# A hybrid encoder layer on one core: SyncE's and ScalarE's orders by hand in the recurrence, and 16 projection steps moved into it

## The chip, the core and the metric

The kernel runs on one core of a Trainium2 chip. TensorE (PE) multiplies, VectorE (DVE) and GpSimd (POOL) do elementwise work, ScalarE (ACT) does copies and activations, and SyncE (SP) issues most of the DMAs; ScalarE's queue issues some too. In the traces each engine takes its instructions in order, and a DMA that is issued on an engine's queue stands in that order as well. The metric is the time of one execution on the device in microseconds: before the change the median of three runs is 1126.07 us (1124.25 to 1127.57).

## What is computed

One layer with two branches is applied to two requests (1024 and 256 positions, 1280 in all, width 1024), with all arithmetic in float32 precision:

```python
h = rmsnorm(x) ; xs, zs, q, k, v, za, gs, ga = split(h @ w_in)      # 5120 columns
ys = s5_bidirectional(xs)            # 32 groups, 64 complex states, both directions
ys = gelu(ys) ; ys *= sigmoid(ys @ w_glu + b_glu) ; ys *= silu(zs)
ya = diff_attention(rotary(q), rotary(k), v)   # 4 heads, softmax1 - lam * softmax2
ya = rmsnorm(ya) * (1 - lam_init) * silu(za)
y  = x + (sigmoid(gs) * (ys @ wb0) + sigmoid(ga) * (ya @ wb1)) @ w_out ; rmsnorm(y)
```

## The kernel before

Float32 products are made of three fp32r products: each operand is split into a high part (a ScalarE cast) and a low part (a subtraction), and `hi*hi + hi*lo + lo*hi` is accumulated in PSUM.

The stages follow one another: norm and V projection; the projections of xs, q and k, with the tables of the recurrence prepared beside them; the recurrence (S5); attention, head by head; the tail behind attention (gate, preparation of both branches, merge, output projection). The 24 remaining projection tiles (zs, za, gs, ga) are no stage of their own: `filler_gen` (L699) is a generator that `fill(n)` (L721) advances by n steps wherever PE would wait. A step is three matmuls of some 424 columns (L706 to L708), eight steps make a chunk in one of two PSUM banks, three chunks make a tile: 576 steps. At a chunk's end ScalarE evicts the bank (`zo`, L712) and issues its store (L713). At the end of a tile's first chunk the weights two tiles ahead are loaded on ScalarE's queue (`w_stage`, L216) and split at once (`w_split`, L233: cast to `wh` at L239 on ScalarE, subtraction to `wl` at L240 on GpSimd). `wh` and `wl` have two buffers, so the cast waits until the tile two before is done.

The recurrence works on 8 blocks of 4 groups. For a block b: `in_mm` has 16 input products on PE (L776, L777), rotations on VectorE (L782 to L785) with two sums each on GpSimd; it also makes the decay table `rt` with four ScalarE activations (L770; two buffers, read by the scans). `scan` has four scans on VectorE (L797, L798) and six products that make `e` (L807 to L812). `out_mm` has 24 output products on PE (L825 to L827) and two gelu activations on ScalarE into `Y` (L828). `store_y` (L831) writes every second block's `Y` with eight DMAs. The order on PE and SP is that of the program (`tc.manual_schedule(engines={PE, SP})`); the other engines' order comes from a planner that simulates the kernel. In program order: loads, `fill(S_PRE=22)`, `in_mm(0)`, `fill(S_LEAD=10)`, and then for each b: loads, `scan(b)`, `in_mm(b+1)`, `fill(S_MID=13)`, `out_mm(b)`, `fill(S_END=4)`: 168 steps.

Attention takes 288 steps. `load_head` (L876) loads a head's q, k and v into the buffers of the recurrence (tags U, tb, mt, wcm, wb) as they come free; for the first head it stands behind the recurrence in the program, outside the hand order, so the planner places its loads among the recurrence's. `unit_scores` makes the scores of a query tile for two softmax terms: the first term needs q0, k00, k10, the second q1, k01, k11; `fill` steps are queued behind each term's score matmuls (L924, L926). The remaining 120 steps are issued by `fill(1000)` in the tail, where the buffers of attention have to come free before `glu_stage` and `ya_stage` can work; the merge products (L1058 to L1060) follow.

Of the kernel before, what the change touches and what calls it, by code (L numbers as in the profile page):

```python
# [11 lines left out]
F32 = mybir.dt.float32  # L12
F32R = mybir.dt.float32r
# [26 lines left out]
S_PRE, S_LEAD, S_MID, S_END = 22, 10, 13, 4  # L40
# [86 lines left out]
def kernel(  # L127
# [570 lines left out]

    def filler_gen():  # L699
        ws = [w_split(w_stage(tiles[0][1], A), G), w_split(w_stage(tiles[1][1], A), G)]  # L700
        for i, (dst, _) in enumerate(tiles):
            wh, wl = ws.pop(0)
            for ci, (c0, n) in enumerate(F_CHUNKS):
                ps = mm_bank()
                for k in range(KD):
                    PE.matmul(ps[:, :n], wh[:, k, :], hTh[:, k, c0:c0 + n], start=(k == 0), stop=False)  # L706
                    PE.matmul(ps[:, :n], wh[:, k, :], hTl[:, k, c0:c0 + n], start=False, stop=False)  # L707
                    PE.matmul(ps[:, :n], wl[:, k, :], hTh[:, k, c0:c0 + n], start=False, stop=(k == KD - 1))  # L708
                    if k < KD - 1:
                        yield  # L710
                zo = wp.tile([128, 512], F32, tag="zo", name="zo", bufs=3)
# [16 lines left out]
    sl = sl_ctx.enter_context(tc.tile_pool(name="s5l", bufs=1, side="right", reuse_waits="tile"))  # L728
    with ExitStack() as p2:
# [34 lines left out]

        def in_mm(b, tb, wb):
            q, gb = b // 2, (b % 2) * NB
            u = U[q]
            rt = sp_.tile([128, NB, J], F32, tag="rt", name="rt", bufs=2)
            for g in range(NB):
                A.activation(rt[:, g], rmask, AF.Copy, scale=r8[:, b * NB + g:b * NB + g + 1])  # L770
# [17 lines left out]
            return rt, bm  # L788
# [46 lines left out]
        with tc.manual_schedule(engines={mybir.EngineType.PE, mybir.EngineType.SP}):  # L835
# [7 lines left out]
            fill(S_PRE)  # L843
            cur = in_mm(0, tbs[0], wbs.pop(0))
            fill(S_LEAD)
            for b in range(NBLK):
# [11 lines left out]
                e = scan(b, tbs.pop(b), *cur)  # L858
# [5 lines left out]
                sig = out_mm(b, wcs.pop(b), e)  # L864
                fill(S_END)
            store_y(3)

    with tc.issue_after(sig.ins):
        tables = A.preload_act_table_set("natural_log_exp_and_others")
    with ExitStack() as p3:  # L870
# [4 lines left out]

        def load_head(h):  # L876
            pr, cb = h // 2, (h % 2) * 2
            big = lambda tag, b: sl.tile([128, NT], F32R, tag=tag, name=f"h{tag}", bufs=b)
            sml = lambda tag, b: sl.tile([128, LL], F32R, tag=tag, name=f"h{tag}", bufs=b)
            q0, k00, q1, vh = big("U", 2), big("tb", 2), big("tb", 2), big("U", 2)  # L880
            k10, k01, k11, vl, rest = sml("mt", 2), sml("wcm", 2), sml("wb", 1), sml("mt", 2), sml("wcm", 2)
            part = lambda i: rest[:, i * LS:(i + 1) * LS]
            v3 = lambda t: t.rearrange("p (k e) -> p k e", e=128)

            def load_q(t, q):
                rows = slice((cb + t) * 32, (cb + t) * 32 + 32)
                for s in range(2):
                    for f in range(2):
                        o = s * 64 + f * 32
                        SP.dma_start(q[o:o + 32].bitcast(F32), q_d[pr][s, f, rows])  # L890

            def load_k(t, hl, k, c0, n):
                rows = slice((cb + t) * 32, (cb + t) * 32 + 32)
                for s in range(2):
                    for f in range(2):
                        o = s * 64 + f * 32
                        SP.dma_start(k[o:o + 32].bitcast(F32), k_d[pr][hl, f, rows, c0:c0 + n])

            load_q(0, q0)
            load_k(0, 0, k00, 0, NT)  # L900
            load_k(0, 1, k10, 0, LL)
            load_q(1, q1)
            load_k(1, 0, k01, 0, LL)
            load_k(1, 1, k11, 0, LL)
            SP.dma_start(v3(vh).bitcast(F32), vh_d[h])
            SP.dma_start(v3(vl).bitcast(F32), vl_d[h][:, 0:8])
            load_k(0, 1, part(0), LL, LS)
            load_k(1, 0, part(1), LL, LS)
            load_k(1, 1, part(2), LL, LS)
            SP.dma_start(v3(part(3)).bitcast(F32), vl_d[h][:, 8:10])  # L910
            return (([q0[:, :LL], q1[:, :LL]], [k00[:, :LL], k01], [k10, k11], v3(vh)[:, 0:8], v3(vl)),
                    ([q0[:, LL:], q1[:, LL:]], [k00[:, LL:], part(1)], [part(0), part(2)],
                     v3(vh)[:, 8:10], v3(part(3))))
# [99 lines left out]
        for h in range(NH):  # L1013
            parts = load_head(h)
# [236 lines left out]
```

## Time and profile before

| | us |
|---|---|
| runs: median, lowest, highest | 1126.07, 1124.25, 1127.57 |
| profiled execution: its time, its span | 1127.2, 1125.1 |
| busy: PE, DVE, ACT, POOL | 1067.2, 801.0, 462.5, 354.8 |
| recurrence: first input product to last output product | 312.2 to 455.2 |
| attention | about 457 to 800 |
| last projection step | 871.2 |

A time in a profile row is counted from the span's start. Rows of a timeline give start, duration, engine, line and tiles; "x8" means that eight instructions in a row are merged, and a bracket tells how long the engine was idle before and which instruction ended that. ACTq and SPq are the queues' own steps, as the issue of a DMA. The granted clock of PE is a share of full speed: 1.0 is 2.4 GHz and 0.5 is 1.2 GHz; its mean over the span is 0.987.

### The profile page before, as it was taken

The numbers are of one execution on the slowest core, as the hardware profiler recorded it, in microseconds if no ns is written. First come the engines' busy times: TensorE is split into PE (matmuls) and PEld (weight loads), VectorE is DVE, ScalarE is ACT, GpSimd is POOL, SyncE is SP. The second block draws the span as 40 slices with busy tenths as digits, with TensorE's granted clock in tenths as the row PEclk, the third lists the DMA queues.
The fourth block names the chain that finished last, engine by engine and source line by source line (L and its number), as shares of the span: only waits on it lengthen the run. The fifth ranks groups of instructions, "written<-read, shape, count | busy, mean of one in ns | idle before, by whom it ended". The sixth has DMA issues, their size and how long they took to land.

```text
span 1125.1 us, 18000 instructions
## 1 busy us (share of the span) xinstructions
PE 1067.2 (95%) x6479; PEld 987.1 (88%) x6479; DVE 801.0 (71%) x1533; ACT 462.5 (41%) x927; POOL 354.8 (32%) x437
## 2 busy tenths in 40 slices
PE   5999799999989999999999999999999999998997
PEld 4878588788979988898999998989999999998997
DVE  5998997888579999478677777766442675666524
ACT  4453222332312121455555645554453445544332
POOL 2447999511032333122122222212141003520032
PEclk9999899999999999999999999999999999999999
DMA  7745453654596676615416316311645975569112
GB/s 212 170 141 188 142 174 117 209 166 156 173 282 174 205 202 168 177 51 150 141 47 169 122 47 186 114 40 60 210 124 174 292 230 128 167 194 270 48 57 94
DMA packets 186154, 173.59 MB, mean 154 GB/s; under 512 B 32721, under 2 KB 161745, under 8 KB 186066
## 3 DMA queue, kind: packets, MB, share of 16 engines
q1 hardware_dynamic: 150738, 144.13, 43.6%
q10 hardware_dynamic: 35328, 28.32, 7.9%
q8 instruction: 51, 0.84, 0.3%
q14 instruction: 37, 0.30, 0.1%
HBM read 113.71 MB, written 58.69 MB: 153 GB/s over the span
## 4 chain that ended last, share of the span: by engine, by line
PE 47%; DVE 18%; DMA 7%; ACT 4%; issue 3%; POOL 2%; SPq 0%; ACTq 0%; POOLq 0%; DVEq 0%
PE mm L706 5%; PE mm L707 5%; PE mm L708 5%; PE xb L1058 3%; PE xb L1059 3%; PE xb L1060 3%; PE pb L246 2%; PE pb L248 2%; PE pb L247 2%; DVE z L797 2%; DVE z L798 2%; PE S L924 2%; DMA yt<-ya_d 2%; PE S L926 2%; DVE mx L928 2%
## 5 line engine op out<-in xcount | busy, mean ns | idle before, releaser
L706 PE MATMUL mm<-hTh,wh 128*128 128x424 f32 (+1 forms) x576 | 212.2, 368 | 6.3 <-ACT zo L712 6.3
L708 PE MATMUL mm<-hTh,wl 128*128 128x424 f32 (+1 forms) x576 | 206.1, 358 | 0.0
L707 PE MATMUL mm<-hTl,wh 128*128 128x424 f32 (+1 forms) x576 | 206.0, 358 | 0.0
L706 PEld LDWEIGHTS mm<-hTh,wh 128*128 128x128 f32 x576 | 109.2, 190 | 12.6 <-ACT zo L712 8.1
L707 PEld LDWEIGHTS mm<-hTl,wh 128*128 128x128 f32 x576 | 109.2, 190 | 4.6
L708 PEld LDWEIGHTS mm<-hTh,wl 128*128 128x128 f32 x576 | 109.0, 189 | 3.4
L928 DVE TENSOR_REDUCE mx<-S 128x1 f32<-128x1024 f32 (+1 forms) x80 | 84.2, 1057 | 38.9 <-PE S L926 38.7
L939 POOL TENSOR_SCALAR p<-p,rs 128x1024 f32<-128x1024 f32 (+1 forms) x40 | 41.7, 1042 | 205.0 <-DVE rs L937 194.2
L246 PE MATMUL pb<-hTh,wh 128*128 128x512 f32 (+1 forms) x288 | 105.7, 367 | 0.0
L247 PE MATMUL pb<-hTl,wh 128*128 128x512 f32 (+1 forms) x288 | 105.1, 365 | 0.0
L932 ACT ACTIVATE p<-S,mx 128x1024 f32<-128x1024 f32 (+1 forms) x80 | 79.2, 992 | 63.0 <-DVE mx L929 53.8
L248 PE MATMUL pb<-hTh,wl 128*128 128x512 f32 (+1 forms) x288 | 103.9, 361 | 0.4 <-DVE wl L240 0.4
L240 POOL TENSOR_TENSOR wl<-wst,wh 128x1024 fp32r<-128x1024 f32 x24 | 64.3, 2679 | 126.5 <-ACT wh L239 51.7
L1191 PE MATMUL tr<-wqh,mh 128*128 128x256 f32 x320 | 89.7, 280 | 1.5 <-DVE o L1195 1.3
L1192 PE MATMUL tr<-wql,mh 128*128 128x256 f32 x320 | 89.3, 279 | 0.0
L1193 PE MATMUL tr<-wqh,ml 128*128 128x256 f32 x320 | 89.0, 279 | 0.0
L248 PEld LDWEIGHTS pb<-hTh,wl 128*128 128x128 f32 x288 | 54.6, 190 | 9.3 <-DVE wl L240 0.9
L246 PEld LDWEIGHTS pb<-hTh,wh 128*128 128x128 f32 x288 | 54.7, 190 | 8.6
L1191 PEld LDWEIGHTS tr<-wqh,mh 128*128 128x128 f32 x320 | 60.1, 188 | 2.4 <-DVE o L1195 2.4
L247 PEld LDWEIGHTS pb<-hTl,wh 128*128 128x128 f32 x288 | 54.6, 190 | 8.4
L1198 POOL TENSOR_TENSOR o<-o,finB 128x256 f32<-128x256 f32 x30 | 27.9, 934 | 103.8 <-ACT jk L1197 103.8
L1192 PEld LDWEIGHTS tr<-wql,mh 128*128 128x128 f32 x320 | 60.1, 188 | 0.0
(387 smaller groups left out, 2793.4 us busy)
## 6 DMA issues: line engine op xcount, KB each, us to landing
wst<-in_w_in_dram ACTq DMA_DIRECT2D x24, 512.0 KB, 4.0
wst<-in_w_in_dram SPq DMA_DIRECT2D x16, 512.0 KB, 4.8
wst<-in_w_branch_dram SPq DMA_DIRECT2D x32, 256.0 KB, 4.4
wqs<-in_w_out_dram SPq DMA_DIRECT2D x16, 512.0 KB, 3.8
tt_d<-tt SPq DMA_DIRECT2D x16, 320.0 KB, 2.6
tb<-tt_d SPq DMA_DIRECT2D x8, 640.0 KB, 5.1
zt<-gs_d SPq DMA_DIRECT2D x16, 320.0 KB, 4.3
x<-in_x_sample_dram SPq DMA_DIRECT2D x8, 512.0 KB, 4.6
```

Source lines behind the costliest of these rows:

```text
L240: e.tensor_tensor(lv, st, hv, op=ALU.subtract)
L246: PE.matmul(ps[:, :n], wh[:, k, :], hTh[:, k, c0:c0 + n], start=(k == 0), stop=False)
L247: PE.matmul(ps[:, :n], wh[:, k, :], hTl[:, k, c0:c0 + n], start=False, stop=False)
L248: PE.matmul(ps[:, :n], wl[:, k, :], hTh[:, k, c0:c0 + n], start=False, stop=(k == KD - 1))
L706: PE.matmul(ps[:, :n], wh[:, k, :], hTh[:, k, c0:c0 + n], start=(k == 0), stop=False)
L707: PE.matmul(ps[:, :n], wh[:, k, :], hTl[:, k, c0:c0 + n], start=False, stop=False)
L708: PE.matmul(ps[:, :n], wl[:, k, :], hTh[:, k, c0:c0 + n], start=False, stop=(k == KD - 1))
L928: V.tensor_reduce(mx, S[:, :nk], axis=AX.X, op=ALU.max)
L932: A.activation(p[:, :nk], S[:, :nk], AF.Exp, bias=mx, scale=1.0 / math.sqrt(HD), accum_out=sm[:, t:t + 1])
L1191: PE.matmul(ps[:, :256], mh[:, k, ts_], oh_[:, k], start=(k == 0), stop=False)
L1192: PE.matmul(ps[:, :256], mh[:, k, ts_], ol_[:, k], start=False, stop=False)
L1193: PE.matmul(ps[:, :256], ml[:, k, ts_], oh_[:, k], start=False, stop=(k == 7))
```

## The change

The order on ScalarE in the recurrence is now that of the program too. The decay tables leave `in_mm`: the first two are made behind `fill(S_PRE)`, table b+2 behind `out_mm(b)`. In the recurrence a weight tile's split is traced apart from its load: at the second step of the next tile (`apart`); during `fill(S_PRE)`, and in attention and the tail, it is traced at once, as before. The first head's loads become a generator `head(0, True)` that is advanced inside the hand order: q0 and k10 ahead of `scan(6)`, k11, k00 and k01 ahead of `scan(7)`, the rest behind the last `store_y`. S_LEAD goes from 10 to 18 and S_MID from 13 to 14, so 184 steps lie in the recurrence and 104 in the tail.

```diff
-S_PRE, S_LEAD, S_MID, S_END = 22, 10, 13, 4
+S_PRE, S_LEAD, S_MID, S_END = 22, 18, 14, 4
     def filler_gen():
         ws = [w_split(w_stage(tiles[0][1], A), G), w_split(w_stage(tiles[1][1], A), G)]
+        st = []
+        def split():
+            with tc.high_priority():
+                ws.append(w_split(st.pop(0), G))
...
+                    if st and (ci, k) == (0, 1):
+                        split()
                 zo = wp.tile([128, 512], F32, tag="zo", name="zo", bufs=3)
                 A.copy(zo[:, :n], ps[:, :n])
                 A.dma_start(dst[:, c0:c0 + n], zo[:, :n])
                 if ci == 0 and i + 2 < len(tiles):
                     with tc.high_priority():
-                        ws.append(w_split(w_stage(tiles[i + 2][1], A), G))
+                        st.append(w_stage(tiles[i + 2][1], A))
+                    if not apart[0]:
+                        split()
...
+    def head(h, staged=False):
...
+        q0 = big("U", 2)
+        load_q(0, q0)
+        if staged:
+            k10 = sml("mt", 2)
+            load_k(0, 1, k10, 0, LL)
+            yield
+            k11, k00, k01 = sml("wb", 1), big("tb", 2), sml("wcm", 2)
+            load_k(1, 1, k11, 0, LL)
+            load_k(0, 0, k00, 0, NT)
+            load_k(1, 0, k01, 0, LL)
+            yield
+            q1 = big("tb", 2)
+            load_q(1, q1)
...
+        vh, vl, rest = big("U", 2), sml("mt", 2), sml("wcm", 2)
...
+        def decay(b):
+            rt = sp_.tile([128, NB, J], F32, tag="rt", name="rt", bufs=2)
+            for g in range(NB):
+                A.activation(rt[:, g], rmask, AF.Copy, scale=r8[:, b * NB + g:b * NB + g + 1])
+            return rt
...
-        with tc.manual_schedule(engines={mybir.EngineType.PE, mybir.EngineType.SP}):
+        with tc.manual_schedule(engines={EN.PE, EN.SP, EN.Activation}):
...
             fill(S_PRE)
+            apart[0] = True
+            rts = [decay(0), decay(1)]
             cur = in_mm(0, tbs[0], wbs.pop(0))
             fill(S_LEAD)
+            first = head(0, True)
             for b in range(NBLK):
...
-                e = scan(b, tbs.pop(b), *cur)
+                if b >= NBLK - 2:
+                    next(first)
+                e = scan(b, tbs.pop(b), rts.pop(0), cur)
...
                 fill(S_MID)
                 sig = out_mm(b, wcs.pop(b), e)
+                if b + 2 < NBLK:
+                    rts.append(decay(b + 2))
                 fill(S_END)
             store_y(3)
+            first = next(first)
+        apart[0] = False
...
-            parts = load_head(h)
+            parts = next(head(h)) if h else first
```

## Rows read from the trace of the kernel before

**Rows 1.** The page, part 1: busy time, share of the span, instructions.
```profile
PE 1067.2 (95%) x6479; PEld 987.1 (88%) x6479; DVE 801.0 (71%) x1533; ACT 462.5 (41%) x927; POOL 354.8 (32%) x437
```
**Rows 2.** PE's waits, 298 to 480 us: total us, times, longest us.
```profile
PE mm L706 <- ACT zo L712: 5.8, 4, 2.3
PE tr L825 <- DVE e L809: 4.8, 1, 4.8
PE S L924 <- ACT p L932: 2.1, 1, 2.1
```
**Rows 3.** Table of stretches, 320 to 440 us: the sum, busy us of each engine.
```profile
sum 120.00, PE 111.46 PEld 107.60 DVE 113.83 ACT 24.15 POOL 39.05; mean PE 18.58 PEld 17.93 DVE 18.97 ACT 4.02 POOL 6.51
```
**Rows 4.** VectorE's timeline in the recurrence: some of the scans.
```profile
318.00 3.65 DVE L797 TENSOR_TENSOR_SCAN z<-rt,bm 64x640 f32<-64x640 f32 x1 [0.34 <-POOL bm L786]
...
404.97 2.15 DVE L797 TENSOR_TENSOR_SCAN z<-rt,bm 64x640 f32<-64x640 f32 x1 [0.33 <-POOL bm L786]
...
420.62 2.13 DVE L797 TENSOR_TENSOR_SCAN z<-rt,bm 64x640 f32<-64x640 f32 x1 [0.33 <-POOL bm L786]
...
427.84 1.49 DVE L798 TENSOR_TENSOR_SCAN z<-rt,bm 64x640 f32<-64x640 f32 x1
...
443.45 3.49 DVE L798 TENSOR_TENSOR_SCAN z<-rt,bm 64x640 f32<-64x640 f32 x1
```
**Rows 5.** GpSimd's timeline, 440 to 470 us: weight splits.
```profile
443.02 2.57 POOL L240 TENSOR_TENSOR wl<-wst,wh 128x1024 fp32r<-128x1024 f32 x1 [3.98 <-ACT wh L239]
458.79 2.39 POOL L240 TENSOR_TENSOR wl<-wst,wh 128x1024 fp32r<-128x1024 f32 x1 [13.20 <-PE S L926]
```
**Rows 6.** Table of stretches, L706 alone: us, PE busy (matmuls), PEld, clock, DMA.
```profile
862.00:871.40 9.40, 5.69 (x16) 2.98 (x16) 1.00 0.54 163
```
**Rows 7.** PE's timeline: first and last output products, scores, first merge product.
```profile
335.00 0.90 PE L825 MATMUL tr<-e,wcm 128*128 128x160 f32 x2 [4.84 <-DVE e L809]
...
341.75 0.46 PE L706 MATMUL mm<-hTh,wh 128*128 128x424 f32 x1
...
452.02 0.43 PE L825 MATMUL tr<-e,wcm 128*128 128x160 f32 x2
...
455.18 0.47 PE L706 MATMUL mm<-hTh,wh 128*128 128x424 f32 x1
...
460.88 0.63 PE L924 MATMUL S<-hwcm,htb 128*128 128x512 f32 x2
...
861.57 0.41 PE L1058 MATMUL xb<-ysh,wh 128*128 128x320 f32 x1 [0.42 <-ACT wh L1051]
```
**Rows 8.** ScalarE's timeline: start of the recurrence, and a store in attention.
```profile
304.92 2.67 ACT L770 ACTIVATE rt<-rmask,r 128x160 f32<-128x160 f32 x8
...
315.59 1.05 ACT L239 CAST wh<-wst 128x1024 fp32r<-128x1024 f32 x1 [6.68 <-PE mm L707]
316.54 0.51 ACT L712 COPY zo<-mm 128x424 f32<-128x424 f32 x1
322.03 0.34 ACTq L713 DMA_DIRECT2D zs_d<-zo  x1
...
468.94 0.33 ACTq L713 DMA_DIRECT2D za_d<-zo  x1
```
**Rows 9.** SyncE's timeline: loads at the recurrence's start and end.
```profile
309.67 11.51 SPq L747 DMA_DIRECT2D mt<-kt_d  x8
...
450.55 1.70 SPq L890 DMA_DIRECT2D htb<-q_d  x4
...
456.25 6.31 SPq L833 DMA_DIRECT2D gy_d<-Y  x8
```
**Rows 10.** Table of stretches: us, PE, PEld, DVE, ACT, POOL, granted clock, DMA.
```profile
334.70:341.50 6.80, 6.27 (x22) 5.87 (x23) 6.71 (x7) 0.44 (x1) 1.37 (x1) 0.50 0.42 155
471.24:474.65 3.41, 3.41 (x13) 2.97 (x11) 1.41 (x3) 0.00 (x0) 0.00 (x0) 0.50 0.14 36
```
**Rows 11.** Loads of q (L890), 430 to 470 us: from issue to landing.
```profile
DMA to landing us min/median/max: 2.6/3.1/5.7
```

More of the change, by code (lines that the diff above doesn't have):

```diff
@@ L697 @@
              + [(gs_d[i], O_GS + i * 128) for i in range(8)] + [(ga_d[i], O_GA + i * 128) for i in range(8)])
+    apart = [False]
     def filler_gen():
         ws = [w_split(w_stage(tiles[0][1], A), G), w_split(w_stage(tiles[1][1], A), G)]
+        st = []
+        def split():
+            with tc.high_priority():
+                ws.append(w_split(st.pop(0), G))
         for i, (dst, _) in enumerate(tiles):
@@ L728, with load_q, load_k @@
     sl = sl_ctx.enter_context(tc.tile_pool(name="s5l", bufs=1, side="right", reuse_waits="tile"))
+    def head(h, staged=False):
+        pr, cb = h // 2, (h % 2) * 2
+        big = lambda tag, b: sl.tile([128, NT], F32R, tag=tag, name=f"h{tag}", bufs=b)
+        sml = lambda tag, b: sl.tile([128, LL], F32R, tag=tag, name=f"h{tag}", bufs=b)
+        part = lambda i: rest[:, i * LS:(i + 1) * LS]
+        v3 = lambda t: t.rearrange("p (k e) -> p k e", e=128)
+        def load_q(t, q):
+            rows = slice((cb + t) * 32, (cb + t) * 32 + 32)
+            for s in range(2):
+                for f in range(2):
+                    o = s * 64 + f * 32
+                    SP.dma_start(q[o:o + 32].bitcast(F32), q_d[pr][s, f, rows])
+        def load_k(t, hl, k, c0, n):
+            rows = slice((cb + t) * 32, (cb + t) * 32 + 32)
+            for s in range(2):
+                for f in range(2):
+                    o = s * 64 + f * 32
+                    SP.dma_start(k[o:o + 32].bitcast(F32), k_d[pr][hl, f, rows, c0:c0 + n])
+        q0 = big("U", 2)
[11 more added lines that the diff above has]
+            load_q(1, q1)
+        else:
+            k00, q1 = big("tb", 2), big("tb", 2)
+            k10, k01, k11 = sml("mt", 2), sml("wcm", 2), sml("wb", 1)
+            load_k(0, 0, k00, 0, NT)
+            load_k(0, 1, k10, 0, LL)
+            load_q(1, q1)
+            load_k(1, 0, k01, 0, LL)
+            load_k(1, 1, k11, 0, LL)
+        vh, vl, rest = big("U", 2), sml("mt", 2), sml("wcm", 2)
+        SP.dma_start(v3(vh).bitcast(F32), vh_d[h])
+        SP.dma_start(v3(vl).bitcast(F32), vl_d[h][:, 0:8])
+        load_k(0, 1, part(0), LL, LS)
+        load_k(1, 0, part(1), LL, LS)
+        load_k(1, 1, part(2), LL, LS)
+        SP.dma_start(v3(part(3)).bitcast(F32), vl_d[h][:, 8:10])
+        yield (([q0[:, :LL], q1[:, :LL]], [k00[:, :LL], k01], [k10, k11], v3(vh)[:, 0:8], v3(vl)),
+               ([q0[:, LL:], q1[:, LL:]], [k00[:, LL:], part(1)], [part(0), part(2)],
+                v3(vh)[:, 8:10], v3(part(3))))
@@ L767, in in_mm @@
             u = U[q]
-            rt = sp_.tile([128, NB, J], F32, tag="rt", name="rt", bufs=2)
-            for g in range(NB):
-                A.activation(rt[:, g], rmask, AF.Copy, scale=r8[:, b * NB + g:b * NB + g + 1])
             bm = sp_.tile([128, 2, NB, J], F32, tag="bm", name="bm", bufs=2)
@@ L787, in in_mm @@
                 G.tensor_tensor(bm[:, 1, gsl], bm[:, 1, gsl], t2, op=ALU.subtract)
-            return rt, bm
+            return bm
         def scan(b, tb, rt, bm):
@@ L874 @@
         grp = [None]
[L876 to L913, printed above, removed]
         def unit_scores(hd, qi, nk, fu):
```

## The prediction

> **What bounds the kernel now.** I read the page first: TensorE (PE) is busy 95% of the span [rows 1], so the time is PE's work plus what PE loses. Its work is the same in both kernels: the 576 projection steps (three matmuls each) are only placed elsewhere. So I looked for where PE loses time. The table of PE's waits between 298 and 480 us [rows 2] shows 4.8 us at the first output product (L825) for VectorE's `e`, 5.8 us in four waits for a ScalarE eviction (`zo`, L712) and 2.1 us at a score matmul (L924). The recurrence is the stretch to ask about.
>
> There VectorE, not PE, sets the pace. The table of stretches over 320 to 440 us has DVE busy 113.8 of 120 us, PE 111.5 [rows 3]. VectorE's timeline shows the blocks as a chain of scans: the block that starts at 404.97 is followed by one at 420.62, 15.65 us later [rows 4]. A block in which a weight split (`wl`, L240) runs on GpSimd is longer: the same scan (L798) takes 1.49 us alone and 3.49 us beside the split that starts at 443.02 [rows 4, 5]. So 15.7 us without a split, 17.7 with one. PE needs less. A projection step is 0.58 us (16 in 9.4 us [rows 6]); 17 of them are 9.9 us; the 24 output products take 3.2 us (452.02 to 455.18 [rows 7]), and the 16 input products at the same rate 2.1: 15.2 us a block. With 18 steps it is 15.8 us, still under VectorE's mean of about 17.2 (three splits in four blocks).
>
> **The change part by part.**
>
> *Sixteen steps move (8 in S_LEAD, 1 in each of 8 S_MID).* They leave the tail behind attention, where the table of stretches counts exactly 16 L706 matmuls, so 16 steps, between 862.0 and 871.4 us [rows 6]: 9.3 us. What is late when they go? The first merge product, at 861.57, waited 0.42 us for a ScalarE cast [rows 7], so the chain of preparations that the tail covers ends just where those 16 steps begin. I take -9.0; the ends are -9.3 and 0 (if that chain grows by as much). In the recurrence the steps fill time in which PE waits for VectorE; that costs nothing as long as VectorE sets the end. If PE set it, they would cost their 9.3 us there.
>
> *Decay tables and ScalarE's hand order, steady blocks.* A block has four `rt` activations, 1.3 us together (eight are 2.67 us [rows 8]). Before, they stood in front of evictions and waited for the scan that frees their buffer; now they follow the output product's gelu, when that scan is long over, and are due a block later. The evictions no longer queue behind them, so the 5.8 us of `zo` waits [rows 2] go. Worth: nothing by itself. The wait for `e` is late next, and VectorE does not wait for PE there.
>
> *Decay tables and hand order, at the start: a loss.* Before, all eight `rt` activations ran from 304.92 on, in time that ScalarE had free [rows 8]. Now their place is behind fill(22). In that fill the split of weight tile 2 is still traced at once, behind the first chunk's eviction and ahead of the second's. Its cast waits until PE has done with tile 0, until 315.59 [rows 8], and the second chunk's eviction, that eviction's store and then the decay tables queue behind it. The store is the trouble. In the trace the eviction of 316.54 is over by 317.05, but its store is issued only at 322.03 [rows 8], after SyncE's eight `mt` loads, issued from 309.67 to 321.18 [rows 9]; ScalarE stood still until then. With the same place in the order the first four tables end at 322.03 + 0.33 + 1.33 = 323.7, against the first scan's start at 318.00 [rows 4]: +5.7 us. If the store is not held, 317.05 + 0.33 + 1.33 = 318.7: +0.7. Off go about 1.5 us: the first scan of 3.65 us, beside the split of tile 2, becomes one of 2.15 us [rows 4], as that split is then over. On come 2.0: the split of tile 8, at 458.79 before [rows 5], moves to step 170, into the last block. For the end of VectorE's last `e` I take +5.0, near the upper end, as the held store stands at this very place in the trace; the ends are -0.8 and +6.2.
>
> Here a rule speaks against the change. The scan beside the split is 2.0 us longer [rows 4, 5]. The Trainium skill (SBUF — State Buffer, Who interferes with whom) says that a VectorE instruction with two SBUF inputs and a GpSimd instruction that reads SBUF exclude each other, and that the loser waits for the whole instruction. By it the split that the extra steps pull into the chain could cost its full 2.6 us [rows 5] instead of 2.0, and the sum would be 0.6 us higher.
>
> *PE at the last output product.* Behind out_mm(6) PE has 4 + 14 steps, 10.4 us, and VectorE a whole block, 17.7 us less the 3.2 us of out_mm(6): PE stands still about 4 us in front of out_mm(7). Before, it idled 2.3 us earlier in that block, at a `zo` [rows 2], and out_mm(7) ran in 3.16 us. Behind its 4.84 us wait out_mm(0) took 6.75 us (335.00 to 341.75 [rows 7]), as the granted clock was 0.50, the 1.2 GHz level, from 334.7 to 341.5 [rows 10]. I take +2.0; the ends are 0 and +3.6.
>
> *First head's loads in SyncE's hand order.* q0 and k10 (8 issues), then k11, k00, k01 (12), come before the last store of Y and are in time. But q1 (4 issues) now stands behind that store, which waits for the last gelu. In the trace q1 was issued at 450.55, before the store's eight issues from 456.25 on [rows 9]. The second score matmul needs q1; it ran at 460.88, 5.7 us behind the end of out_mm(7) at 455.18 [rows 7]. New: the store starts 1.07 us behind out_mm(7) as before, eight issues at 0.43 us (q1's four took 1.70) make 3.4, four more 1.7, and q1 lands 3.1 us later (the median of these loads [rows 11]): 9.3 us behind out_mm(7). PE waits 3.6 us and cannot use the time, as the next steps are queued behind that matmul. With about 1.6 us for a low clock behind it: +5.2. Ends: +2.0 (landing in 2.6 us, and PE reaching the matmul later on a low clock) and +11 (rival B). Queued behind q1 are vh, vl and 13 small loads, needed only at the first attention output and for the short sequence.
>
> *The old stall in attention.* PE waited 2.1 us for an exp [rows 2] that stood on ScalarE behind a `za_d` store, issued only at 468.94 [rows 8] amid SyncE's last small loads of the head, and then ran 3.4 us at clock 0.50 [rows 10], about 1.6 us lost. Chunks now end at other steps (184 and 192), so the store that met those loads is elsewhere, and I let the stall go: -3.7, with 0 as the other end.
>
> **Sum** against the profiled execution of 1127.2 us (span 1125.1): -9.0 + 5.0 + 2.0 + 5.2 - 3.7 = -0.5, so 1126.7. The median of the runs, 1126.07, is 1.1 lower; on its scale I forecast 1125.6 us. About 0.3% (3.4 us) is what a measurement of this kernel tells from no change, so this is the same time: what the tail gives, the start and the end of the recurrence take.
>
> **Rivals.**
> - *A, the first decay tables are in time and the recurrence ends where it did.* The store is issued without a hold, the first scan starts by 318.7 (+0.7), the split of tile 8 meets no scan and out_mm(7) no low clock: -9.0 + 0.7 + 5.2 - 3.7 = -6.8, 1119.3 us. For it: one ScalarE store is gone from among the loads of the start, which may land earlier. Against it: the hold until 322.03 is in the trace at just this place.
> - *B, q1 becomes the bound (slower).* The store's eight issues take 6.31 us, as in the trace [rows 9], and q1 lands after 5.7 us, the longest of these loads [rows 11]: it is there 14.8 us behind out_mm(7), PE waits 9.1 us, and with the low clock behind it that is +11: -9.0 + 5.0 + 2.0 + 11 - 3.7 = +5.3, 1131.4 us. It decides from about 12 us between out_mm(7) and the second score matmul. Against it: in the trace the large vh load was in flight beside that store; now it comes later.
> - *C, the tail's cover is missing.* The gate and attention-output preparation, which starts only when attention ends, takes a few us longer with other splits among it, and PE idles at the first merge product: half of the 9 us is lost, +4.0 in all, 1130.1 us. For it: that chain ends within 2 us of where the fill would end. Against it: the removed steps bring no instruction to it.
>
> **Chances.** Forecast 0.42, A 0.27, B 0.20, C 0.11. The forecast's spread (about 4 us) puts 0.06 of it on the fast side and 0.04 on the slow side; a few hundredths of A, B and C fall within 0.3%: faster 0.31, same 0.40, slower 0.29. Range: all terms at their good ends give 1115, at their bad ends 1137 and more; to hold 8 in 10 it takes in most of A and B: 1118.5 to 1132.5. As cases of both signs hold over half, the likeliest one's own range: 1121.5 to 1129.5.
>
> **What would show it.** The first scan starts near 323, with ScalarE idle ahead of the first `rt` (A: by 319). PE has no `zo` wait beyond the first block; it waits at L825 for `e`, in the last block with the clock at 0.50 behind it. The last `e` ends near 457 us. The second score matmul comes over 9 us behind out_mm(7), released by a q_d load. The last projection step ends within 1 us of the first merge products. The forecast is wrong if the last `e` ends by 453 (PE, not VectorE, gained), or if q1 is there when PE asks.

## The result, and the profile after

The changed kernel takes 1138.26 us (median of 4 runs, 1135.4 to 1139.39) against 1126.82 us in the same session: ratio 1.010, 95% interval 1.0072 to 1.0129, so 1.0% slower. The profiled execution took 1137.24 us, its span 1135.5, against 1127.2 and 1125.1. The prediction was 1125.6 us (1118.5 to 1132.5): 12.7 us too fast, and the measured time lies 5.8 us above the range.

The page of the kernel after has as many matmuls as before and 5 us more of PE's busy time (a projection matmul of 0.36 us took 0.56 us at the lower clock); the rest is idle time [rows 1].

```profile
PE 1072.5 (94%) x6479; PEld 991.0 (87%) x6479; DVE 806.9 (71%) x1533; ACT 464.6 (41%) x927; POOL 352.6 (31%) x437
```

PE's waits of the kernel after, 298 to 480 us (total us, times, longest):

```profile
PE mm L714 <- ACT zo L722: 5.2, 2, 3.7
PE tr L894 <- issue: 4.3, 2, 3.4
PE S L963 <- DMA htb<-q_d: 2.2, 1, 2.2
```

The steady `zo` waits [rows 2] are gone: the two of 5.2 us stand in the first block, before 327 us. New is the wait at the last output products (3.4 us; the profile names no releaser; the first half of the last `e` is finished just ahead of it, at 456.90) and the one for q1 (`htb<-q_d`). ScalarE's timeline at the start shows the held store, and VectorE's the first scan (line 866 is 797 of before):

```profile
317.29 0.51 ACT L722 COPY zo<-mm 128x424 f32<-128x424 f32 x1
323.03 0.35 ACTq L723 DMA_DIRECT2D zs_d<-zo  x1
323.43 2.34 ACT L834 ACTIVATE rt<-rmask,r 128x160 f32<-128x160 f32 x7 [5.63 <-DMA mt<-kt_d]
```
```profile
324.90 1.48 DVE L866 TENSOR_TENSOR_SCAN z<-rt,bm 64x640 f32<-64x640 f32 x1 [6.51 <-ACT rt L834]
...
449.02 3.57 DVE L867 TENSOR_TENSOR_SCAN z<-rt,bm 64x640 f32<-64x640 f32 x1
...
456.82 0.82 DVE L881 TENSOR_TENSOR e<-e,f 128x640 f32<-128x640 f32 x1
```

This is the start as forecast: the store is held for 5.2 us, the profile puts the end of that down to the landing of an `mt` load, the first scan starts at 324.90 instead of 318.00 [rows 4], the last block's scan meets the split (3.57 us), and the last `e` ends at 457.6, 5.6 us later than before. Then PE's timeline at the last output products and the scores, and SyncE's beside it:

```profile
457.00 0.38 PE L894 MATMUL tr<-e,wcm 128*128 128x160 f32 x1 [3.36 <-issue]
...
462.13 0.47 PE L714 MATMUL mm<-hTh,wh 128*128 128x424 f32 x1
...
473.58 0.70 PE L963 MATMUL S<-hwcm,htb 128*128 128x512 f32 x2 [2.17 <-DMA htb<-q_d]
```
```profile
462.90 4.13 SPq L902 DMA_DIRECT2D gy_d<-Y  x8
467.13 1.79 SPq L754 DMA_DIRECT2D htb<-q_d  x4
```

out_mm(7) ends 6.95 us later than before [rows 7] and takes 5.1 us, most of it at the lower clock; q1 is issued behind the store of Y, where it was issued ahead of it before [rows 9], and the first score product with q1 comes 11.4 us behind out_mm(7) (5.7 before). The table of stretches gives the granted clock (the column with 0.50, the 1.2 GHz level) behind both waits:

```profile
457.28:460.70 3.42, 3.34 (x13) 3.01 (x12) 0.36 (x1) 0.00 (x0) 0.00 (x0) 0.50 0.05 12
474.35:477.76 3.41, 3.41 (x11) 3.15 (x10) 1.38 (x3) 1.20 (x2) 0.00 (x0) 0.50 0.44 128
```

All that had been priced. What had not been is the attention. PE's timeline has the first product with vh of each head (L1000; L961 before), first of the kernel after, then of before:

```profile
493.25 0.28 PE L1000 MATMUL tr<-wTh,hU 128*128 128x256 f32 x1
...
576.83 0.28 PE L1000 MATMUL tr<-wTh,hU 128*128 128x256 f32 x1
...
661.45 0.28 PE L1000 MATMUL tr<-wTh,hU 128*128 128x256 f32 x1
...
745.97 0.28 PE L1000 MATMUL tr<-wTh,hU 128*128 128x256 f32 x1
```
```profile
484.34 0.28 PE L961 MATMUL tr<-wTh,hU 128*128 128x256 f32 x1
...
567.33 0.28 PE L961 MATMUL tr<-wTh,hU 128*128 128x256 f32 x1
...
645.79 0.28 PE L961 MATMUL tr<-wTh,hU 128*128 128x256 f32 x1
...
728.78 0.28 PE L961 MATMUL tr<-wTh,hU 128*128 128x256 f32 x1
```

Three heads take 244.4 us before and 252.7 after. So the 10.4 us of span come from four places: +8.9 up to the first of these products, +8.3 in three heads, -1.7 in the fourth head, and -5.1 behind the last of them (794.1 to the end at 1125.1; 809.6 to 1135.5). PE's waits in attention, 480 to 800 us, after and then before, name most of the heads' loss (the transposes at L988 read the merged `p`, which is ready at 565.00 in the first of them; the profile names `mx`, which ends just behind it):

```profile
PE tr L988 <- DVE mx L968: 8.2, 5, 2.3
PE tr L1000 <- DVE mx L968: 1.7, 3, 0.6
```
```profile
PE S L924 <- ACT p L932: 3.7, 5, 1.0
PE tr L949 <- DVE wTl L953: 1.4, 2, 0.7
```

A stall of 2.3 us at the transposes of `p` (L988) comes back at 565.05, 648.05 and 732.63, and behind the second and third the clock is at 0.51 (3.5 us each):

```profile
648.40:651.90 3.50, 3.50 (x14) 3.32 (x13) 3.45 (x8) 3.02 (x6) 1.12 (x1) 0.51 0.27 68
733.70:737.20 3.50, 3.50 (x12) 3.22 (x11) 3.18 (x8) 2.31 (x6) 1.12 (x1) 0.51 0.24 59
```

GpSimd's timeline at the first of them, and VectorE's:

```profile
557.74 2.51 POOL L240 TENSOR_TENSOR wl<-wst,wh 128x1024 fp32r<-128x1024 f32 x1 [14.70 <-ACT wh L239]
560.24 1.57 POOL L978 TENSOR_SCALAR p<-p,rs 128x1024 f32<-128x1024 f32 x1
```
```profile
557.31 0.68 DVE L1032 SCALAR_TENSOR_TENSOR ya<-ya,rr 128x512 f32<-128x512 f32 x1
557.91 0.16 DVE L976 RECIPROCAL rs<-sm 128x2 f32<-128x2 f32 x1
...
558.03 2.77 DVE L1033 SCALAR_TENSOR_TENSOR ya<-ya,rr 128x512 f32<-128x512 f32 x1
...
560.84 1.50 DVE L1034 TENSOR_TENSOR ya<-ya 128x512 f32<-128x512 f32 x1
562.26 1.21 DVE L967 TENSOR_REDUCE mx<-S 128x1 f32<-128x1024 f32 x1
563.39 0.41 DVE L1013 TENSOR_TENSOR ya<-ya 128x256 f32<-128x256 f32 x1
563.73 1.27 DVE L979 SCALAR_TENSOR_TENSOR p<-p,rs,p 128x1024 f32<-128x1024 f32 x1
```

`rs` is there from 558.1, but GpSimd splits a weight tile until 560.25, and the product p·rs (L978) queues behind it; VectorE's norm product L1033, like L1032 in shape, takes 2.77 us instead of 0.68 beside the split. The merge of p (L979) starts 5.7 us behind `rs`, and PE waits at the transposes. The queue on GpSimd is not what ends last: p·rs is done at 561.81, while VectorE is in L1034 until 562.34. VectorE is late by the 2.1 us of L1033, and by another 1.5 us because the planner's order has a reduction of the next scores (L967) and L1013 ahead of the merge. The Trainium skill (SBUF — State Buffer, Who interferes with whom) says that a VectorE instruction with two SBUF inputs contends with a GpSimd instruction that reads SBUF, and that the port pair they share is an exclusive lock; the trace agrees: L1033 ends at 560.80, 0.55 us behind the split, and so nearly waited for all of it.

Why in every head? A head issues 72 steps (8 units of 7 and 2 of 8), three whole weight tiles of 24. So the split would meet each head at the same place, and the steps ahead of attention set which: 168 before, seven tiles exactly; 184 after, seven and two thirds. That was the theory to test.

### The profile page after: what moved, and what is told of

Its sections match the earlier page's. It is cut to its first block, busy times and chain, and to the rows that moved or that the text cites. A ratio compares the mean times of both kernels' runs of the same rounds, so it can differ in the third digit from the quotient of the medians.

```text
span 1135.5 us, 17995 instructions
## 1 busy us (share of the span) xinstructions
PE 1072.5 (94%) x6479; PEld 991.0 (87%) x6479; DVE 806.9 (71%) x1533; ACT 464.6 (41%) x927; POOL 352.6 (31%) x437
## 4 chain that ended last, share of the span: by engine, by line
PE 49%; DVE 16%; DMA 8%; issue 3%; POOL 2%; ACT 2%; SPq 1%; ACTq 0%; POOLq 0%; DVEq 0%
PE mm L714 5%; PE mm L715 5%; PE mm L716 5%; PE xb L1097 3%; PE xb L1098 3%; PE xb L1099 3%; DVE z L866 3%; PE tr L988 2%; PE S L963 2%; DVE z L867 2%; PE pb L246 2%; PE pb L248 2%; PE pb L247 2%; PE S L965 2%; DMA yt<-ya_d 2%
## 5 line engine op out<-in xcount | busy, mean ns | idle before, releaser
L967 DVE TENSOR_REDUCE mx<-S 128x1 f32<-128x1024 f32 (+1 forms) x80 | 84.3, 1059 | 46.6 <-PE S L965 45.7
L978 POOL TENSOR_SCALAR p<-p,rs 128x1024 f32<-128x1024 f32 (+1 forms) x40 | 42.6, 1064 | 213.8 <-DVE rs L976 205.9
L722 ACT COPY zo<-mm 128x424 f32<-128x424 f32 (+1 forms) x72 | 36.9, 512 | 86.9 <-PE mm L716 82.2
```

The source lines that it names most:

```text
L967: V.tensor_reduce(mx, S[:, :nk], axis=AX.X, op=ALU.max)
```

## The experiments

Each ratio is against runs of the kernel before in the same session. The columns (us, from PE's timelines) are: start of the first product with vh; three heads; fourth head; from the last attention product to the end; span. The columns are of one profiled execution each, which lies up to 3.5 us from the median of its kernel's runs; the ratios go by all runs.

| kernel | ratio (95%) | first vh | 3 heads | 4th | rest | span |
|---|---|---|---|---|---|---|
| before (168 steps) | 1 | 484.3 | 244.4 | 65.3 | 331.0 | 1125.1 |
| after (184) | 1.010 (1.0072–1.0129) | 493.3 | 252.7 | 63.6 | 325.9 | 1135.5 |
| after, 168 | 1.0096 (1.0080–1.0111) | 492.8 | 245.4 | 65.2 | 333.0 | 1136.4 |
| after, 192 | 1.0038 (1.0020–1.0055) | 496.6 | 245.3 | 64.0 | 322.5 | 1128.3 |
| after, q1 first | 1.0027 (1.0014–1.0040) | 487.2 | 252.8 | 63.7 | 326.2 | 1129.9 |
| after, loads back | 1.0023 (1.0012–1.0034) | 487.9 | 255.2 | 63.7 | 324.5 | 1131.2 |
| after, 8 more at entry | 0.9990 (0.9977–1.0002) | 496.8 | 244.5 | 63.9 | 323.4 | 1128.5 |
| after, no splits | 0.9971 (0.9957–0.9986) | 491.1 | 242.4 | 64.7 | 326.7 | 1124.9 |
| after, 168, no splits | 0.9984 (0.9972–0.9996) | 493.2 | 236.9 | 63.3 | 331.9 | 1125.3 |
| before, 176 | 1.0062 (1.0041–1.0083) | 494.4 | 248.6 | 61.6 | 329.3 | 1134.0 |
| before, 184 | 0.9988 (0.9972–1.0003) | 484.2 | 252.9 | 63.7 | 324.8 | 1125.5 |
| before, 184 and 8 at entry | 0.9944 (0.9923–0.9965) | 489.0 | 245.0 | 64.0 | 324.4 | 1122.3 |
| before, 192 (26, 14) | 0.9926 (0.9911–0.9941) | 485.0 | 245.0 | 64.0 | 323.8 | 1117.7 |
| before, 192 (18, 15) | 0.9919 (0.9905–0.9934) | 486.0 | 244.5 | 64.0 | 322.8 | 1117.3 |
| before, 184, VectorE splits | 0.9894 (0.9879–0.9909) | 484.9 | 242.9 | 64.3 | 324.8 | 1117.0 |
| before, 192 (18, 15), VectorE splits | 0.9853 (0.9828–0.9878) | 487.6 | 237.8 | 63.0 | 321.4 | 1109.8 |

**The steps undone.**
```diff
-S_PRE, S_LEAD, S_MID, S_END = 22, 18, 14, 4
+S_PRE, S_LEAD, S_MID, S_END = 22, 10, 13, 4
```


> The changed kernel with the step counts of before (S_LEAD 10, S_MID 13: 168 steps ahead of attention). What is to be explained: TensorE's lost time between 480 and 800 us is 20.0 us in the changed kernel and 11.3 in the one before, with a stall of 2.4 us in each head at L988. Theory P (phase): a head issues 72 steps, three whole weight tiles of 24, so each head meets the weight splits at the same places; 168 is seven tiles, 184 is seven and two thirds, which puts a split on GpSimd just ahead of the product p times rs. Then the 2.4 us stalls go and the attention's loss falls to about 11 us; 16 steps (9.3 us) come back to the tail; the last e ends some 2 us earlier: 1138.3 - 8.7 + 9.3 - 2 = about 1137 us. Theory O (order): the late q1 made the order of scores of the first units another one, and that lasts for all heads. Then the stalls stay and the time is 1138.3 + 9.3 - 2 = about 1145.5 us.

1138.87 us; the heads are back at 245.4 us and the 2.3 us stalls are gone. As theory P had it; the hand order of the loads (theory O) does not make the heads slow. Against before, the hand orders alone cost 11.3 us of span: 8.5 up to the first vh, the rest spread.

**The steps alone**, in the kernel before.
```diff
-S_PRE, S_LEAD, S_MID, S_END = 22, 10, 13, 4
+S_PRE, S_LEAD, S_MID, S_END = 22, 18, 14, 4
```


> The kernel before with the new step counts alone (S_LEAD 18, S_MID 14). Theory P: the attention loses about 20 us instead of 11.3, with a stall of over 2 us in each head, while 9.3 us leave the tail and the recurrence gains or loses up to 2 us: 1126.8 - 9.3 + 8.7 = about 1126 us, up to 1130 with the later losses of the merge. Theory O: the order of the scores is that of before, the attention loses 11 to 12 us, and the time is 1126.8 - 9.3 + 2 = about 1119.5 us.

1126.81 us, the heads 252.9: P again. Up to the first vh nothing is lost (484.2) though 16 steps more are done there, but that is a balance: out_mm(7) ends 2.6 us later than before, and the old stall with its low clock is gone. So the 16 steps cost the recurrence 2.6 us here (1.6 in the changed kernel, against its version with 168 steps) and not their 9.3: PE had room for most of them, as the prediction had it. What leaves the tail (-6.2) the heads take (+8.5).

**q1 first.**
```diff
             load_q(1, q1)
+            yield
...
+            next(first)
             store_y(3)
```


> The changed kernel with the four loads of q1 ahead of the last store of Y in SyncE's hand order, nothing else. Both theories: q1 is there when TensorE asks, and the 2.3 us wait at the fourth score product with the clock of 0.50 behind it goes: -3 to -4 us at the entry to attention. Theory P: the stalls of 2.4 us in each head stay, about 1135 us. Theory O: the scores come in the order of before, the stalls go too, and the time is about 1126 us.

1131.1 us: the first vh comes 6.1 us earlier, the heads stay at 252.8. The late q1 is one cost, the phase another.

**192 steps in the changed kernel.**
```diff
-S_PRE, S_LEAD, S_MID, S_END = 22, 18, 14, 4
+S_PRE, S_LEAD, S_MID, S_END = 22, 26, 14, 4
```


> The changed kernel with eight steps more (S_LEAD 26): 192 steps ahead of attention, eight whole weight tiles. Theory P: the splits fall in each head where they fell before; the 2.4 us stalls go, the attention loses about 11 us instead of 20; 4.7 us more leave the tail, up to that much comes on in the first block: 1138.3 - 8.7 = about 1129.5 us, between 1125 and 1131. Theory O: no change in attention, 1134 to 1139 us.

1131.7 us, the heads 245.3: the stall goes with more steps as well as with fewer, which tells a phase from an amount. The time is 2 us over the value named and 0.7 over its range; the first vh came 3.3 us later.

**The first decay tables ahead of the fill.**
```diff
+            rts = [decay(0), decay(1)]
             fill(S_PRE)
             apart[0] = True
-            rts = [decay(0), decay(1)]
```


> The changed kernel with the first two blocks' decay tables put ahead of fill(S_PRE) in ScalarE's hand order, nothing else. If VectorE sets the recurrence's end, as the prediction had it: the first scan starts by 319.5 us instead of 324.9, the last e ends 4 to 5.5 us earlier (near 452.5), and the time is 1138.3 - 5 = about 1133.5 us, with the stalls of 2.4 us in each head unchanged. Rival: with 18 and 14 steps TensorE sets the end; the first scan is early, but the last output product still ends near 461, and the time stays at 1137 to 1139 us.

1146.02 us (1.015, 1.0133 to 1.0167), against both expectations, and by an effect of the edit's own: a load of the filler's weights, issued on ScalarE, moved behind the tables (304.29), the next one was issued only at 319.43, and PE waited 10.0 us for `wh`. It says nothing of who sets the end.

**The loads out of the hand order.**
```diff
-            first = head(0, True)
...
-                if b >= NBLK - 2:
-                    next(first)
...
-            first = next(first)
...
-            parts = next(head(h)) if h else first
+            parts = next(head(h))
```


> The changed kernel with the first head's loads taken out of SyncE's hand order again (issued as the other heads' are, in the order that the planner finds); 184 steps, the decay tables and ScalarE's hand order stay. If the loads' hand order costs by the late q1: the wait for q_d and the clock of 0.50 behind it go, 1138.3 - 7 = about 1131 us, as with q1 put first; the stalls of 2.4 us in each head stay, since 184 steps do. If its cost is in the order of the other loads too, it is below 1129 us. If the hand order of loads has no part in it: 1137 to 1139 us.

1131.92 us: 5.4 us earlier at the first vh, the heads as slow (255.2). What is left between this and the steps alone is 3.7 us at the first vh. The late first tables do not make it: the first scan starts 5.8 us later here (324.87 against 319.11), yet the last `e` ends at the same time (454.8 against 454.7). What is later is out_mm(7), by 4.1 us; ahead of it PE waits 4.0 us, until 450.0, for a `zo`, an eviction in ScalarE's hand order.

**192 steps in the kernel before.**
```diff
-S_PRE, S_LEAD, S_MID, S_END = 22, 10, 13, 4
+S_PRE, S_LEAD, S_MID, S_END = 22, 26, 14, 4
```


> The kernel before with 24 more steps (S_LEAD 26, S_MID 14: 192 ahead of attention, eight whole weight tiles) and nothing else of the change. Theory P (phase): the stalls of 2.4 us in each head, which the 16 steps alone had (TensorE lost 28.5 us between the first score and the last attention output against 22.1), are absent, and 14 us leave the tail: between 1117 and 1122 us. If the stalls come from having more steps ahead of attention at all, they are there and the time is 1124 to 1128 us.

1121.14 us, 0.9926, heads 245.0. The phase decides in this kernel too. But of 14 us of steps only 7.2 are gained behind attention. PE's waits from 850 us on show a part:

```profile
PE xb L1058 <- DVE zt L1172: 4.9, 3, 3.8
PE xb L1058 <- ACT yah L1051: 1.8, 1, 1.8
```

An early merge product now waits 1.8 us for the cast of `yah`, where before there was no such wait: rival C's mechanism, at 24 steps. The waits for `zt` are 1.6 us longer than before (3.3), and at 1020.5 us, near the longest of them, the granted clock falls to 0.50 for 6.8 us; in the kernel before it stays at 1.0 there.

**The split later.**
```diff
-        apart[0] = False
```


> The changed kernel (184 steps) with the weight splits of attention 18 steps later than their load, as in the recurrence (the line that sets apart back is gone). The steps of projection stand where they did; only the cast and the split of the next weight tile move against them. Theory P in its narrow form (the split on GpSimd stands ahead of the product p times rs and beside VectorE's norm): the 2.4 us stalls at L988 in each head go or shrink below 1 us, and the time falls by 5 to 8 us, to about 1131.5 us. In its wide form (the phase of the steps themselves, their evictions and chunk ends, is what costs): the stalls stay, 1137 to 1139 us.

1134.21 us (1.0050, 1.0032 to 1.0068); heads 252.9, span 1135.6. The edit did not move what it was to move: the cast of a weight tile waits until PE is done with the tile in its buffer, so the split stood at the same place (556.68, 2.51 us). It tells nothing between the forms of P. Its median is 4 us below the changed kernel's, which the spans (1135.6 and 1135.5) do not show; the cause is open.

**No splits in attention.**
```diff
+    bare = [False]
...
         def split():
             with tc.high_priority():
+                if bare[0]:
+                    h, l = w_pair_tiles()
+                    A.copy(h, st.pop(0))
+                    G.memset(l.bitcast(F32), 0.0)
+                    ws.append((h, l))
+                else:
-                ws.append(w_split(st.pop(0), G))
+                    ws.append(w_split(st.pop(0), G))
...
+        bare[0] = True
```
GpSimd fills the low part with zeros, which leaves out a part of the products.

> The changed kernel (184 steps) in which, from the first attention unit on, GpSimd fills wl with zeros in place of the weight split (this leaves out the low part of the later weight tiles); the cast of the high part and all steps stand. Theory P in its narrow form (the split of 2.5 us stands ahead of the product p times rs on GpSimd and beside VectorE's norm, which takes 2.77 us instead of 0.69): the 2.4 us stalls at L988 in each head go or shrink below 1 us, and the time falls by 5 to 9 us to about 1131 us. In its wide form (the phase of the steps, evictions and chunk ends): the stalls stay, 1136 to 1139 us.

1126.13 us, and the stalls of 2.3 us are gone, as the narrow form had it; the gain of 12 us is more than it named. At the same unit GpSimd's and VectorE's timelines (lines 8 further down) now read:

```profile
555.30 0.96 POOL L711 MEMSET wl<- 128x1024 f32 x1 [14.67 <-PE mm L723]
556.63 1.56 POOL L986 TENSOR_SCALAR p<-p,rs 128x1024 f32<-128x1024 f32 x1 [0.37 <-DVE mx L976]
```
```profile
556.38 0.16 DVE L984 RECIPROCAL rs<-sm 128x2 f32<-128x2 f32 x1
...
556.50 0.68 DVE L1041 SCALAR_TENSOR_TENSOR ya<-ya,rr 128x512 f32<-128x512 f32 x1
...
558.65 1.27 DVE L987 SCALAR_TENSOR_TENSOR p<-p,rs,p 128x1024 f32<-128x1024 f32 x1
```

The norm product takes 0.68 us, the merge of p starts 2.1 us behind `rs` instead of 5.7, and PE does not wait. In this kernel the planner has the merge directly behind the norm's products, so of the 3.6 us gained here 2.1 are the product's and 1.5 VectorE's order.

**All three costs mended**: q1 first as above, the tables as in the next run, and
```diff
-S_PRE, S_LEAD, S_MID, S_END = 22, 18, 14, 4
+S_PRE, S_LEAD, S_MID, S_END = 22, 26, 14, 4
```


> The changed kernel with its three costs taken out together: 192 steps (S_LEAD 26), q1 loaded ahead of the last store of Y, and the first two blocks' decay tables behind the second step of fill(S_PRE). If the three costs are separate ones, 1138.3 - 6.6 (192 steps) - 4 (q1, as far as it isn't in the 192 steps already) - 4 (tables) = about 1123.5 us, between 1118 and 1127. If the start term is not to be had, because TensorE then sets the end: 1126 to 1129 us.

1131.28 us (1.0022, 1.0008 to 1.0037), over both ranges: the tables' new place cost as much as it gave, 9.4 us of PE's wait for a `zo`, as the next run shows alone.

**The tables behind two steps.**
```diff
-            fill(S_PRE)
+            fill(2)
+            rts = [decay(0), decay(1)]
+            fill(S_PRE - 2)
             apart[0] = True
-            rts = [decay(0), decay(1)]
```


> The changed kernel with the first two blocks' decay tables behind the second step of fill(S_PRE), so that the first weight tiles' loads and casts stay ahead of them; nothing else. If VectorE sets the recurrence's end: the first scan starts by 319.5 us instead of 324.9, the last e ends 3 to 5.5 us earlier, and the time is about 1134 us, with the 2.4 us stalls in attention unchanged. If TensorE or the splits set it: the last e ends near 456 as it did, 1137 to 1139 us.

1138.17 us (1.0068, 1.0041 to 1.0095). The first scan starts at 319.56, yet the last `e` ends 2.6 us later than in the changed kernel. ScalarE's timeline has the next thing that is late:

```profile
312.99 0.38 ACTq L218 DMA_DIRECT2D wst<-in_w_in_dram  x1
324.16 1.04 ACT L239 CAST wh<-wst 128x1024 fp32r<-128x1024 f32 x1 [15.41 <-DMA wst<-in_w_in_dram]
```

The load of weight tile 2 lands after 11.2 us, its cast stands ahead of an eviction in ScalarE's order, and PE waits 9.0 us for that. So the start's 5 us are not had by moving the tables; no version here mends it.

**176 steps in the kernel before.**
```diff
-S_PRE, S_LEAD, S_MID, S_END = 22, 10, 13, 4
+S_PRE, S_LEAD, S_MID, S_END = 22, 10, 14, 4
```


> The kernel before with 8 steps more (S_MID 14: 176 ahead of attention, seven and a third weight tiles), nothing else. Theory P: the splits fall at a third set of places in each head, neither those of 168 and 192 steps nor those of 184; the attention's loss is another constant per head (the stalls repeat every 84 us), and the time lies between 1119 us (no worse than 168: 4.7 us leave the tail, some idle time in the recurrence is filled) and 1130 us. Without a phase, by interpolation between 168 steps and 184 steps in this kernel: 1127 us.

1136.77 us, above both. The heads take 248.6, a third phase between the others. The rest is another cost: PE waits 11.4 us, until 447.4, for a `k_d` load of the first head. SyncE issues a store of Y ahead of that load, but so it does with 184 steps, where PE waited 0.4 us for it. What differs is PE: here the first score product stands ahead of out_mm(6), with 184 steps behind it. So this time shows how much the place of the first score products can cost, and is no measure of the phase.

**Eight steps at the entry of attention**, in the changed kernel and, with 18 and 14 (184 steps), in the kernel before.
```diff
-F_PRE = 0
+F_PRE = 1
```


> The changed kernel with 8 steps at the head of attention, ahead of the first score product (F_PRE 1): the recurrence stays at 184 steps, the units of attention stand in the phase of 192. If the phase is what made attention slower: the 2.4 us stalls at L988 go, the loss between 480 and 800 us falls from 20 to about 11 us, and the 4.7 us of steps cover the wait for q1: between 1122 and 1130 us. If the 184 steps of the recurrence themselves change the attention: the stalls stay, 1134 to 1138 us.

> The kernel before with S_LEAD 18, S_MID 14 (184 steps) and the same 8 steps at the head of attention. Phase as with 192 steps: no 2.4 us stalls, 1126.8 - 6 = about 1121 us, beside the 1121.1 us of the kernel with all 192 steps in the recurrence. If it is over 1125 us, the place of the 8 steps matters and not the phase alone.

1126.85 and 1122.09 us; heads 244.5 and 245.0, without the 2.3 us stalls. The recurrence has 184 steps in both: the phase at the entry alone decides.

**No splits, with 168 steps**: the zeros in place of the splits, as above, and
```diff
-S_PRE, S_LEAD, S_MID, S_END = 22, 18, 14, 4
+S_PRE, S_LEAD, S_MID, S_END = 22, 10, 13, 4
```


> The changed kernel with the step counts of before (168 steps) in which GpSimd fills wl with zeros in place of the weight splits from the first attention unit on (the low part of the later weight tiles is left out). It says what the splits cost in the phase of before: with 184 steps their absence gave 11 to 12 us. If the place of the splits is what the 184 steps made worse, their absence gives less here, 3 to 6 us (1138.9 to about 1134 us); if splits cost the same in any phase, 11 to 12 us again (about 1127.5 us).

1126.93 us, 12 us less: the splits cost the same in this phase, and my narrow form is not the whole of it. Three heads take 236.9 us without splits and 245.4 with them at 168 steps, 242.4 and 252.7 at 184: the splits cost 8.5 to 10.3 us in either phase, and the phase 5.5 to 7.3 us with or without splits. (With the fourth head, where a few matmuls fall to the other side of a column's border, it is 9.3 and 10.4 us for the splits, 5.7 and 6.8 for the phase.) PE's waits in the three heads without splits, at 184 steps and then at 168, show what else the phase moves:

```profile
PE S L971 <- DMA htb<-q_d: 1.8, 1, 1.8
PE mm L721 <- ACT zo L729: 0.9, 2, 0.4
PE S L971 <- DMA htb<-k_d: 0.5, 1, 0.5
```
```profile
PE S L971 <- ACT p L979: 0.2, 1, 0.2
```

In the phase of 184 evictions (`zo`) and the next head's loads meet the units too; where the split is away, these are late next, some 3 of the 5.5 us. The 2.3 us stall is the split's; that the heads of 184 are slower is the phase's, which moves splits, evictions and loads together. Which of these costs how much in each head is not shown.

**192 steps put otherwise**, in the kernel before.
```diff
-S_PRE, S_LEAD, S_MID, S_END = 22, 10, 13, 4
+S_PRE, S_LEAD, S_MID, S_END = 22, 18, 15, 4
```


> The kernel before with 192 steps put otherwise (S_LEAD 18, S_MID 15 in place of 26 and 14). Phase theory: attention as with the other 192, no 2.4 us stalls; the recurrence's blocks of 19 steps are 16.4 us of TensorE against VectorE's mean of some 17.2, so its end comes at most 2 us later and the first block gives 2 us back: 1119 to 1124 us. If TensorE becomes the bound of the blocks: 1125 us or more.

1119.49 us, its ratio within 0.1% of the other 192's.

**The splits of attention on VectorE**, in the kernel before with 192 and with 184 steps.
```diff
+    late = [G]
...
-                        ws.append(w_split(w_stage(tiles[i + 2][1], A), G))
+                        ws.append(w_split(w_stage(tiles[i + 2][1], A), late[0]))
...
+        late[0] = V
         fill(F_PRE * KD)
```


> The kernel before with 192 steps (S_LEAD 18, S_MID 15) and the weight splits of attention on VectorE instead of GpSimd; all is computed. Without any split the attention of the 168-step kernel lost 9 us less. If what a split costs is GpSimd's turn (p times rs behind it, 2.5 us), most of that is saved: 1119.5 - 6 = about 1114 us. If VectorE, busy 61 of 83 us in a head, pays for it in the chain of p instead: 1119 to 1123 us.

> The kernel before with 184 steps (S_LEAD 18, S_MID 14) and the weight splits of attention on VectorE. If the bad phase is that of a split on GpSimd, the 2.4 us stalls at L949 of the 184 steps are absent, and the time is within 6 us above that of the 192 steps with the same change: about 1118 us against 1126.8 with the splits on GpSimd. If the phase costs on any engine: 1124 to 1128 us.

1111.54 and 1117.0 us: 1.5% and 1.1% faster than the kernel before, with everything computed. PE's waits in attention (480 to 800 us) with 192 steps, then with 184:

```profile
PE tr L951 <- DVE mx L931: 0.5, 1, 0.5
```
```profile
PE tr L951 <- DVE p L942: 2.9, 3, 1.0
PE mm L708 <- ACT zo L714: 1.8, 4, 0.4
```

In the good phase the heads go from 244.5 to 237.8 us, nearly as if there were no splits: more than was named, and not for the reason named. In the traces with 168 and 192 steps no p·rs stands behind a split on GpSimd, so GpSimd's turn is not what the splits cost there. What they meet is VectorE's products. With 192 steps and the splits on GpSimd, GpSimd's timeline and then VectorE's read:

```profile
519.46 3.16 POOL L240 TENSOR_TENSOR wl<-wst,wh 128x1024 fp32r<-128x1024 f32 x1 [2.10 <-ACT wh L239]
```
```profile
520.27 2.90 DVE L992 TENSOR_TENSOR ya<-ya,rr 128x512 f32<-128x512 f32 x1
...
600.67 3.20 DVE L940 SCALAR_TENSOR_TENSOR p<-p,rs,p 128x1024 f32<-128x1024 f32 x1
```

L992 takes 0.68 us elsewhere and the merge of p (L940) 1.27; in three heads VectorE's instructions beside a split take 6.8 us more than alone. With the splits on VectorE, 1.22 us each, that is gone. How much of the gain comes from it is not shown. The stall in the phase of 184 shrinks from 2.3 to 1.0 us, and the phase still costs 5.1 us (242.9 against 237.8). The kernel with 192 steps and the splits on VectorE is the fastest of all.

## Why the prediction was wrong

- *Up to attention: right, in part by a balance.* The terms +5.0, +2.0, +5.2 and -3.7 make 8.5 us up to the first product with vh; it came 8.9 us later. In its parts this is a balance: the first score product with q1 came 12.7 us later (10.6 by the terms), and from there to the first product with vh 3.8 us were made good (2.1 by the terms). Each was seen: the held store at 323.03, the last `e` at 457.6 (457 forecast), out_mm(7) 2 us longer at the lower clock, and the first score product with q1 behind q_d, though two terms with q0 had come ahead of it. By itself q1 was worth 6.1 us (forecast 5.2). The 16 steps cost the recurrence 1.6 to 2.6 us at the end of out_mm(7), about the 2.0 booked for the split of tile 8. The first scan came 6.9 us late (forecast 5.7), of which the first block gave back 3.2 (forecast 1.5).
- *The rule on VectorE and GpSimd* was weighed in the recurrence, where it was to add 0.6 us at most (the scan beside the split grew by 2.1 us, near the 2.0 of the rows, and not by 2.6). It mattered in attention, where I did not look.
- *The step that failed* is the old stall in attention. It says that chunks now end at other steps, and books the one gain of that at the entry. The same shift moves the splits, evictions and loads in all four heads, which the sum holds at nothing: +8.3 in three heads, -1.7 in the fourth. Without these 6.6 us the time would lie in the range, near its slow end. The trace of before had what was needed: 72 steps a head against 24 a tile, so that what a tile brings (split, eviction, store) stands at fixed places in each head.
- *The tail was mis-sized.* -9.0 was booked and -5.1 came behind attention (-6.8 with the fourth head). The loss is not where rival C has it: from the last attention product to the first merge product (867.48, 861.57 before) the time fell by 9.6 us, so up to there the steps were worth their full length. (The last step does not end within 1 us of that product, as was forecast: 16 steps still run among the merge products in both kernels, until 877.4 and 871.5.) Behind it 4.5 us are lost: in waits for `zt` (5.3 us against 3.3 before; ScalarE's `zt` activations wait there for loads of gs_d), and in 3.4 us at clock 0.50 from 1041.0 on; before, it was 1.0 there. What makes those loads late was not tested. With 192 steps a part of the loss has rival C's cause (`yah`, 1.8 us).
- Together: +0.4 up to attention, +6.6 in it, +3.9 behind it are the 10.9 us between the sum of -0.5 and the 10.4 of the spans.

## What to carry to other kernels

Where filler work is dealt out in a fixed number of steps per unit, its period against the units' period says whether a cost repeats: moving steps in one stage moves every later filler event, and the count has to be taken modulo that period before any term is booked. Look at what runs on the other engine beside the short two-input products of the chain (here a 0.68 us product took 2.77 us beside a 2.5 us split), and at the order in which their own engine has them; moving the splits to VectorE gave 0.7% here, re-dealing the steps 0.8%. An engine whose queue looks late need not be the one that is waited for last. And a step taken from a tail is worth its length only while the chain beneath it is shorter.

## What the runs showed of the hardware that was not expected

The exclusion goes both ways. Beside GpSimd's split VectorE's 0.68 us product took 2.77 us; in the run with 184 steps and the splits on VectorE, GpSimd's p·rs, 1.12 to 1.16 us elsewhere, took 2.53 us beside a VectorE split of 1.22 us that had started 0.2 us earlier. GpSimd's memset of the same tile (0.96 us) slowed nothing on VectorE.
